# First mixer of a diffusion trunk: the scans' small PSUM tiles alternate between two banks, one of them the bank of the finishing transposes

## The chip, the cores and the metric

The kernel is one program on one core of a Trainium2 chip. The metric is the device time of one execution in microseconds (us). Before the change it is 3440.08 us, the median of three runs (3439.80 to 3440.29). The core's engines are PE (TensorE: matmuls and transposes), DVE (VectorE), ACT (ScalarE), POOL (GpSimd) and SP (SyncE, which here only issues DMAs). Each runs its own queue of instructions strictly in order and waits for the others on semaphores.

## The reference, cut to what matters

The trunk has two layers over 1280 tokens (256 of a prompt and 1024 latents). The change lies in the mixer of the first one, which runs two scans beside each other, each forwards and backwards, on one input projection:

```python
def mlstm_scan(q, k, v, log_i, log_f, C0, n0, m0):
...
        s = jnp.einsum('bthd,bshd->btsh', qc, kc) * jnp.exp(dmat - m_t[:, :, None, :])
        w_inter = jnp.exp(inter - m_t)
        num = jnp.einsum('btsh,bshv->bthv', s, vc) + w_inter[..., None] * jnp.einsum('bthd,bhdv->bthv', qc, C)
...
        C = keep[..., None, None] * C + jnp.einsum('bsh,bshd,bshv->bhdv', wg, kc, vc)
...
def ssd_scan(x, dt, A, Bm, Cm, S0):
...
        w = jnp.einsum('btgn,bsgn->btsg', Cc, Bc)[..., None] * decay * dtc[:, None]
        y = (jnp.einsum('btsgr,bsgrp->btgrp', w, xc)
             + jnp.einsum('btgn,bgrpn->btgrp', Cc, S) * jnp.exp(acum)[..., None])
...
        S = jnp.exp(a_last)[..., None, None] * S + jnp.einsum('bsgr,bsgrp,bsgn->bgrpn', wS, xc, Bc)
...
def even_mixer(h, w_in, ...):
...
    qk, v, o, ig, fg, z, xbc, dt = _split(h @ w_in, EVEN_SIZES)
    qk = jax.nn.silu(dwconv(qk, conv_a_w, conv_a_b)).astype(F32)
...
    ha = group_rms(ha, NH_A, a_norm_w).astype(h.dtype)
...
    yb = group_rms(y, NG_B, b_norm_w).astype(h.dtype)
    out = jnp.concatenate([ha, yb], axis=-1) @ w_out
```

Behind it stand an MLP, the second layer's attention mixer and another MLP, which the change does not touch.

## The kernel before

`Even.run` computes the first mixer. It walks through four pairs of scans: `ssd(0)`, `mlstm(0)`, `ssd(1)`, `mlstm(1)` and so on; an `ssd(i)` is two heads of the state-space scan, an `mlstm(h)` one head of the other. Each scan takes the 1280 tokens in ten chunks of 128 and both directions at once. In a first pass over the chunks, `key(c)` transposes the keys of a chunk on PE (tile `pk` or `pb`), ACT scales them out of PSUM, and `state(c)` multiplies them into the chunk's contribution to the state. In a second pass, `weights(c)` computes the 128x128 product of queries and keys (`pS` or `pG`), DVE multiplies it into the decay matrix of that chunk (`bcm` or `bcs`: sent by DMA, masked by DVE, exponentiated by ACT), and one step later `rows(c-1)` multiplies the matrix of the chunk before with the values (`pn` or `pny`). `ssd` also transposes the start states (`s0p`) and, when the second pass has reached the end of a direction, the final state (`sfp`, `final`), which ACT copies out (`so`).

When a group of four chunks (or the last two) has all its rows, it is normalised and `finish` transposes it (`fps`, up to four transposes into one bank), and ACT scales it out (`ob`); the last mLSTM head and the last SSD pair instead split it into two parts for the next matmul (ACT `hh`, then DVE `hl`).

Between all these small steps PE runs the input projection of what comes next: `self.gap()` pulls a few matmuls (`mmf`, `mmt`) out of `self.stream` after each step. PE's order there is written out by hand, since the scheduler is told to leave PE alone:

```python
            with net.pool("eu2") as self.u2, net.pool("es") as self.sp:
                with self.tc.manual_schedule(engines=PE_ONLY):
                    for i in range(4):
                        j = i // 2
```

The orders of ACT, DVE, POOL and SP are the scheduler's. After the block, the second pass of the last head, `mlstm(3, X)`, runs as `for _ in self.last: self.gap()`, and there the scheduler orders PE too. That stretch, about 725 to 794 us of the trace, is called the tail here; it ends where the output projection's matmuls (`o`) begin.

PSUM has eight banks of 512 fp32 columns. The pool of this mixer, opened as `net.pool("eps", 1, psum=True)`, gives three to the projection (tag `mm`), two to the rows (`n`), one to the states (`c`), one to the finishing transposes (`tp`: `fps`, `sfp`), and one to the small tiles (`s`: `pk`, `pS`, `s0p`, `pb`, `pG`). A tag with one buffer means that the next tile of the tag may be written only when the last reader of the one before has finished. Line numbers are those of the kernel before; from L1475 on, the changed kernel's are 4 higher.

Of the kernel before, what the change touches and what calls it, by code (L numbers as in the profile page):

```python
# [9 lines left out]
F32 = mybir.dt.float32  # L10
# [6 lines left out]
P = 128  # L17
# [978 lines left out]
class Even:  # L996
# [18 lines left out]
    def proj_feat(self, hi, lo, m, sink):  # L1015
        for g, (o, n, s) in enumerate(GROUPS):
            ps = self.pp.tile([P, 512], F32, tag="mm", name="mmf", bufs=3)
            self.net.gemm(ps[:m, :n], lambda k: (hi[:, k, :m], lo[:, k, :m]), lambda k: self.h[g][k], range(KD))
            sink(g, ps[:m, :n])

    def w_feat(self, col):
        hi = self.wp.tile([P, KD, P], F32R, tag="wh", name="wf_hi")
        lo = self.wp.tile([P, KD, P], F32R, tag="wl", name="wf_lo")
        raw = self.raw([P, KD, P])
        self.nc.sync.dma_start(raw, self.a["w_in_even"][0, :, col:col + P].rearrange("(k p) f -> p k f", p=P))
        self.split_w(raw, hi, lo)
        return hi, lo
# [431 lines left out]
    def mlstm(self, h, X=None):  # L1459
        nc, V, sp, pp = self.nc, self.nc.vector, self.sp, self.pp  # L1460
# [14 lines left out]
        kw = {}  # L1475

        def key(c):
            pk = pp.tile([P, 512], F32, tag="mm", name="pk", bufs=3) if X else pp.tile([P, P], F32, tag="s", name="pk", bufs=1)
            nc.tensor.transpose(pk[:, :P], kT[:, c * P:(c + 1) * P], self.net.ident)
            kw[c] = sp.tile([P, 2, P], F32, tag="kw", name="kw", bufs=2)  # L1480
            for d in range(2):
                nc.scalar.activation(kw[c][:, d, :], pk[:, :P], AF.Copy, scale=col(1, d, c))
# [22 lines left out]

        def weights(c):
            p0 = c * P
            pS = pp.tile([P, P], F32, tag="s", name="pS", bufs=1)
            nc.tensor.matmul(pS, kT[:, p0:p0 + P], qT[:, p0:p0 + P], start=True, stop=True)
            b = bc[c]  # L1510
            V.tensor_tensor(b[:, 0], pS.unsqueeze(1).to_broadcast([P, 2, P]), b[:, 0], ALU.mult)
            (nc.gpsimd if BQ else V).tensor_tensor(b[:, 1], qT[:, p0:p0 + P].unsqueeze(1).to_broadcast([P, 2, P]), b[:, 1], ALU.mult)
# [23 lines left out]
        for c in range(NT + 1):  # L1536
            if c < NT:
                key(c)
                yield 1
            if c > 0:  # L1540
                state(c - 1)
                yield 1
# [29 lines left out]
    def ssd(self, i):  # L1572
        net = self.net
        nc, V, sp, pp = self.nc, self.nc.vector, self.sp, self.pp
# [11 lines left out]
        for q in range(0, NT, 3):  # L1586
            ps = pp.tile([P, 3, P], F32, tag="n", name="xps", bufs=2)
# [6 lines left out]
            self.gap(XG)  # L1594
        for d in range(2):
            c0, c1 = ORDERS[d][0][0], ORDERS[d][1][0]
            ps = pp.tile([P, P], F32, tag="s", name="s0p", bufs=1)
            nc.tensor.transpose(ps, s0[:, d], self.net.ident)
            nc.scalar.copy(S[d][:, c0, :], ps)
            nc.gpsimd.memset(S[d][:, c1, :], 0.0)  # L1600
            self.gap(XG)
# [2 lines left out]
        bt, xw = {}, {}  # L1604

        def key(c):
            pb = pp.tile([P, P], F32, tag="s", name="pb", bufs=1)
            nc.tensor.transpose(pb, BT[:, c * P:(c + 1) * P], self.net.ident)
            bt[c] = sp.tile([P, P], F32, tag="bt", name="bt", bufs=2)
            nc.scalar.copy(bt[c], pb)  # L1610
            xw[c] = sp.tile([P, 2, 2, 64], F32, tag="kw", name="xw", bufs=2)
            (nc.gpsimd if XW else V).tensor_tensor(xw[c], x4(c), cb(c, 2), ALU.mult)
# [12 lines left out]
        for c in range(NT + 1):  # L1625
            if c < NT:
                key(c)
                self.gap()
            if c > 0:
                state(c - 1)  # L1630
                self.gap()
# [25 lines left out]

        def weights(c):
            p0 = c * P
            pG = pp.tile([P, P], F32, tag="s", name="pG", bufs=1)  # L1660
            nc.tensor.matmul(pG, BT[:, p0:p0 + P], CT[:, p0:p0 + P], start=True, stop=True)
            b4 = bc[c].rearrange("p d h t -> p (d h) t")
            V.tensor_tensor(b4, b4, pG.unsqueeze(1).to_broadcast([P, 4, P]), ALU.mult)
            xd[c] = sp.tile([P, 2, 2, 64], F32, tag="xd", name="xd", bufs=2)
            (nc.gpsimd if XD else V).tensor_tensor(xd[c], x4(c), cb(c, 1), ALU.mult)
# [62 lines left out]
    def run(self, fills=((), (), (), ())):  # L1728
        nc, net = self.nc, self.net
        self.wp = net.enter(net.pool("ew", EW, side="right"))  # L1730
        with net.pool("eu") as self.up, net.pool("ec") as cp, net.pool("eps", 1, psum=True) as self.pp:
            slots = cycle(range(4))
            u = lambda: self.up.tile([P, T], F32, tag=f"u{next(slots)}", name="raw_u", bufs=1)
            rings = cycle((lambda: self.raw([P, D]), lambda: u()[:, :D]))
            self.h = net.first(lambda: next(rings)(), self.pp)
            self.free, self.U, self.where, self.held, self.todo = list(range(4)), {}, {}, [], []
            self.pulled = self.done = 0
            self.credit = self.ratio = 0.0
            B = lambda j: self.channel("B", 2576 + 512 + j * P, 12 + j, self.bcs[j, 0])
            C = lambda j: self.channel("C", 2576 + 768 + j * P, 14 + j, self.bcs[j, 1])  # L1740
            x = lambda i: self.channel("x", 2576 + i * P, 8 + i)
            q = lambda i: self.channel("q", i * P, i)
            k = lambda i: self.channel("k", 512 + i * P, 4 + i)
            items = [B(0), x(0), C(0)]
            need, self.zdone = [], []
            for i in range(4):
                need.append(len(items) - (i % 2 == 0))
                items += [self.project_zv(i), q(i), k(i)]
                self.zdone.append(len(items) - 2)
                need.append(len(items))  # L1750
                if i % 2 == 0:
                    items += [self.project_o(i // 2), x(i + 1)]
                elif i == 1:
                    items += [B(1), x(2), C(1)]
            steps = self.adas(fills[2])
            items[MIX[0]:] = [self.mixed(t, steps, MIX[1]) for t in items[MIX[0]:]]
            items += [self.rest(steps), (lambda: None, self.early)]
            self.work = self.stream(items)
            with net.pool("er") as rp:
                self.setup(cp, self.pp, rp)  # L1760
                self.gates(rp)
                self.rows_ssd(rp)
                self.rows_mlstm(rp)
                nc.sync.dma_start(self.KS, self.keepd.partition_broadcast(P))
            self.pull(PULL)
# [4 lines that stand above are left out]
                        self.finish_items(need[2 * i])  # L1770
                        self.ratio = RATIO[2 * i]
                        if i % 2:
                            nc.sync.dma_start(self.take("C"), self.bcs[j, 1])
                        self.ssd(i)
                        self.finish_items(need[2 * i + 1])
                        self.ratio = RATIO[2 * i + 1]
                        if i % 2 == 0:
                            nc.sync.dma_start(self.take("B"), self.bcs[j, 0])
                        if i < 3:
                            for w in self.mlstm(i):  # L1780
                                self.gap(w)
                    while self.pull(1):
                        pass
                    while self.todo:
                        self.gap()
                for _ in self.last:
                    self.gap()
                while self.todo:
                    self.gap()
                us = iter(self.free[:NU])  # L1790
                u = lambda: next((self.up.tile([P, T], F32, tag=f"u{q}", name="ox_raw", bufs=1) for q in us), None) or self.u2.tile([P, NT, 130], F32, tag="C", name="ox_raw", bufs=CB).rearrange("p c f -> p (c f)")[:, :T]
                if OB == 1:
                    net.out_begin(self.a["w_out_even"][0], self.mixo, EVEN_K, 5, lambda: self.raw([P, D]), u)
                for _ in self.adas(FILLS[4], True):
                    pass
                if OB == 0:
                    net.out_begin(self.a["w_out_even"][0], self.mixo, EVEN_K, 5, lambda: self.raw([P, D]), u)
                net.leave(1)
# [818 lines left out]
```

## Time and profile before

| | |
|---|---|
| median of three runs | 3440.08 us (3439.80 to 3440.29) |
| the profiled execution | 3443.51 us, its span 3441.7 us |
| mean granted clock of PE in it | 0.975 |
| first mixer's scans, manual part | about 120 to 725 us of the span |
| its tail, to the output projection | about 725 to 794 us |
| the rest (output projection, MLP, second layer) | 794 to 3441.7 us |

The profiled execution is one single run and 3.4 us longer than the median. All durations below come from it. The trace's clock is a share of PE's full speed: 1.00 stands for 2.4 GHz and 0.50 for 1.2 GHz.

### The profile page before, as it was taken

How to read it: one execution, taken by the hardware profiler on the slowest of the kernel's cores; microseconds unless marked ns; L12 is line 12 of the kernel's file. 1: busy time of each engine (PE TensorE's matmuls, PEld its weight loads, DVE VectorE, ACT ScalarE, POOL GpSimd, SP SyncE). 2: the span in 40 equal slices, each digit the busy share in tenths (PEclk: the TensorE clock that was granted, in tenths of full speed). 3: DMA queues.
4: the chain of work that ended last, by engine and by line, in shares of the span. 5: the costliest groups of instructions: out<-in, count | busy, mean ns of one | idle time of the engine just before them, and what ended most of it. 6: DMA issues, size and time to landing. Idle time of an engine off the chain costs nothing. (4 is left out here: it accounts for less than half of the span.)

```text
span 3441.7 us, 50028 instructions
## 1 busy us (share of the span) xinstructions
PE 3250.1 (94%) x17997; PEld 2645.0 (77%) x17997; DVE 2236.0 (65%) x4130; ACT 1635.7 (48%) x3829; POOL 603.7 (18%) x977
## 2 busy tenths in 40 slices
PE   7898989979999999999969999999999999999998
PEld 4788778857888888888748776666678888888887
DVE  4665856664588877787635366666655866656666
ACT  4444544444544444434534466555555444444443
POOL 2323432321111110001211142000001111100112
PEclk8999999979999999999979999999999999999999
DMA  6334343265345546664432221000143443355544
GB/s 213 74 102 115 98 137 94 81 162 174 110 154 183 173 174 219 185 196 152 154 113 72 74 68 35 1 9 8 39 158 113 160 147 137 136 194 173 159 136 174
DMA packets 319460, 435.25 MB, mean 126 GB/s; under 512 B 29900, under 2 KB 210476, under 8 KB 319212
## 3 DMA queue, kind: packets, MB, share of 16 engines
q1 hardware_dynamic: 296620, 343.17, 32.5%
q0 software_dynamic: 22592, 88.89, 6.8%
q8 instruction: 141, 2.31, 0.3%
q14 instruction: 107, 0.88, 0.1%
HBM read 309.55 MB, written 122.43 MB: 126 GB/s over the span
## 5 line engine op out<-in xcount | busy, mean ns | idle before, releaser
L193 PE MATMUL y<-oph 128*128 128x512 f32 x896 | 348.7, 389 | 1.7 <-DVE y L724 1.7
L195 PE MATMUL y<-oph,opl 128*128 128x512 f32 x896 | 348.6, 389 | 0.0
L194 PE MATMUL y<-opl,oph 128*128 128x512 f32 x896 | 348.6, 389 | 0.0
L199 DVE TENSOR_TENSOR opl<-sa,oph 128x512 fp32r<-128x512 f32 x216 | 158.8, 735 | 167.2 <-ACT oph L198 166.9
L198 ACT CAST oph<-sa 128x512 fp32r<-128x512 f32 x216 | 133.9, 620 | 259.3 <-PE y L194 178.0
L193 PEld LDWEIGHTS y<-oph 128*128 128x128 f32 x896 | 168.2, 188 | 37.2 <-DVE y L724 2.1
L194 PEld LDWEIGHTS y<-opl,oph 128*128 128x128 f32 x896 | 168.2, 188 | 35.1
L195 PEld LDWEIGHTS y<-oph,opl 128*128 128x128 f32 x896 | 168.2, 188 | 34.8
L479 POOL DMA_DIRECT2D hd<-x x96 | 52.2, 544 | 645.5 <-ACT x L481 497.2
L193 PE MATMUL mmf<-hh,wf_hi 128*128 128x512 f32 (+1 forms) x384 | 152.5, 397 | 0.0
L1065 DVE SCALAR_TENSOR_TENSOR u<-pre,cw,u 128x510 f32<-128x510 f32 (+2 forms) x192 | 145.4, 766 | 9.7 <-ACT u L1063 8.5
L193 PE MATMUL mmt<-wt_hi,hh 128*128 128x256 f32 x480 | 149.7, 312 | 0.0
L194 PE MATMUL mmf<-hl,wf_hi 128*128 128x512 f32 (+1 forms) x384 | 139.3, 363 | 0.0
L195 PE MATMUL mmf<-hh,wf_lo 128*128 128x512 f32 (+1 forms) x384 | 139.3, 363 | 0.0
L194 PE MATMUL mmt<-wt_lo,hh 128*128 128x256 f32 x480 | 137.5, 286 | 0.0
L195 PE MATMUL mmt<-wt_hi,hl 128*128 128x256 f32 x480 | 137.3, 286 | 0.0
L204 POOL TENSOR_SCALAR rs_v<-ss 128x1 f32<-128x1 f32 x85 | 30.1, 354 | 496.6 <-ACT junk L956 347.6
L193 PE MATMUL o<-wh,hh 128*128 128x512 f32 x280 | 112.0, 400 | 0.0
L194 PE MATMUL o<-wl,hh 128*128 128x512 f32 x280 | 109.3, 390 | 0.7 <-DVE wl L199 0.7
L195 PE MATMUL o<-wh,hl 128*128 128x512 f32 x280 | 109.5, 391 | 0.0
L1993 PE MATMUL pom<-PTm,mla_h 128*64 128x256 f32 x336 | 106.5, 402 | 2.4 <-DVE ob L2005 2.0
L405 ACT ACTIVATE x<-x 128x512 f32<-128x512 f32 x112 | 70.3, 628 | 78.7 <-DVE x L638 60.5
(1081 smaller groups left out, 10240.3 us busy)
## 6 DMA issues: line engine op xcount, KB each, us to landing
sa<-hd SPq DMA_DIRECT2D x108, 512.0 KB
hd<-s POOLq DMA_DIRECT2D x128, 320.0 KB, 3.0
hd<-x POOLq DMA_DIRECT2D x96, 320.0 KB, 2.5
wh<-in_w_down SPq DMA_DIRECT2D x40, 512.0 KB
wl<-in_w_down SPq DMA_DIRECT2D x40, 512.0 KB
w_raw<-in_w_ada SPq DMA_DIRECT2D x32, 512.0 KB
wh<-in_w_up SPq DMA_DIRECT2D x30, 512.0 KB
wl<-in_w_up SPq DMA_DIRECT2D x30, 512.0 KB
```

What stands on the lines that cost most here:

```text
L193: mm(ps, lh, rh, start=first and j == 0, stop=False)
L194: mm(ps, lh, rl, start=False, stop=False)
L195: mm(ps, ll, rh, start=False, stop=last and j == n - 1)
L198: self.nc.scalar.copy(hi, raw)
L199: self.nc.vector.tensor_tensor(lo, raw, hi.bitcast(F32), ALU.subtract)
L204: nc.gpsimd.tensor_scalar(v, ss, scale, eps, ALU.mult, ALU.add)
L405: relu = lambda o, i: nc.scalar.activation(o, i, AF.Relu)
L479: store = lambda i, z: nc.gpsimd.dma_start(hd[p, i], z)
L1065: nc.vector.scalar_tensor_tensor(us, pre[:, i:i + e - a], cw[:, b, j + i:j + i + 1], us, ALU.mult, ALU.add)
L1993: self.nc.tensor.matmul(self.po[64 * b:64 * b + 64, 0], self.odd.Vm[(0 if self.big else 10) + 2 * i + b][:, 64 * self.h:64 * self.h + 64], ...
```

## The change

A new method hands out the small tiles. Each is a whole bank, of which the first 128 columns are used, and its tag alternates: the first tile goes to `s`, the second to `tp`, the third to `s`, whatever the tile is. `fps` and `sfp` stay on `tp` and are not counted in the turns.

```diff
@@ class Even
+    def small(self, name):
+
+        return self.pp.tile([P, 512], F32, tag=next(self.banks), name=name, bufs=1)[:, :P]
+
...
-            pk = pp.tile([P, 512], F32, tag="mm", name="pk", bufs=3) if X else pp.tile([P, P], F32, tag="s", name="pk", bufs=1)
+            pk = pp.tile([P, 512], F32, tag="mm", name="pk", bufs=3) if X else self.small("pk")
...
-            pS = pp.tile([P, P], F32, tag="s", name="pS", bufs=1)
+            pS = self.small("pS")
...
-            ps = pp.tile([P, P], F32, tag="s", name="s0p", bufs=1)
+            ps = self.small("s0p")
...
-            pb = pp.tile([P, P], F32, tag="s", name="pb", bufs=1)
+            pb = self.small("pb")
...
-            pG = pp.tile([P, P], F32, tag="s", name="pG", bufs=1)
+            pG = self.small("pG")
...
             self.pulled = self.done = 0
+            self.banks = cycle(("s", "tp"))
             self.credit = self.ratio = 0.0
```

PE's instructions and their order stay the same up to the tail; only what they wait for changes. On ACT, DVE, POOL and SP the scheduler moves some instructions by a few places throughout the mixer.

The first place is PE in the second pass of `mlstm(0)`: the small tile of one chunk, a step of projection, and the rows of the chunk before. Before:

```order
L195 MATMUL mmf_2717<-hh0_6_297,wf_lo_2241 128x512
L1509 MATMUL pS_2787<-u_1791,u_2096 128x128 [waits DVE_49]
L193 MATMUL mmf_2717<-hh0_7_299,wf_hi_2240 128x512
L194 MATMUL mmf_2717<-hl0_7_300,wf_hi_2240 128x512
L195 MATMUL mmf_2717<-hh0_7_299,wf_lo_2241 128x512
L1517 MATMUL pn_2806<-vx_2255,bcm_2673 128x129 [waits Activation_49]
```

And now:

```order
L195 MATMUL mmf_2717<-hh0_6_297,wf_lo_2241 128x512
L1513 MATMUL pS_2787<-u_1791,u_2096 128x128 [waits PE_49]
L193 MATMUL mmf_2717<-hh0_7_299,wf_hi_2240 128x512
L194 MATMUL mmf_2717<-hl0_7_300,wf_hi_2240 128x512
L195 MATMUL mmf_2717<-hh0_7_299,wf_lo_2241 128x512
L1521 MATMUL pn_2806<-vx_2255,bcm_2673 128x129 [waits DVE_49,Activation_49]
```

Nothing moved; the wait for DVE's multiplication went from the small tile to the rows behind it.

The second place is PE in the second pass of `ssd(0)`, where the final state's transpose `sfp` stands directly before a small tile `pG`, whose turn is `tp`. Before:

```order
L195 MATMUL mmf_1812<-hh1_4_421,wf_lo_1238 128x512
L1692 MATMUL sfp_1853<-ident_60,finS_1217 128x128 [waits Activation_49]
L1661 MATMUL pG_1866<-u_1138,u_895 128x128 [waits DVE_49]
L193 MATMUL mmf_1812<-hh1_5_423,wf_hi_1237 128x512
L194 MATMUL mmf_1812<-hl1_5_424,wf_hi_1237 128x512
```

And now:

```order
L195 MATMUL mmf_1812<-hh1_4_421,wf_lo_1238 128x512
L1696 MATMUL sfp_1853<-ident_60,finS_1217 128x128 [waits PE_49,Activation_49]
L1665 MATMUL pG_1866<-u_1138,u_895 128x128 [waits Activation_49]
L193 MATMUL mmf_1812<-hh1_5_423,wf_hi_1237 128x512
L194 MATMUL mmf_1812<-hl1_5_424,wf_hi_1237 128x512
```

Nothing moved; `pG` now waits for ACT, which is the copy of the `sfp` in front of it. The same stands at all eight `sfp` and, with `pS`, `pb` or `pk` behind `fps`, at most of the finishing transposes.

The third place is PE in the tail, at its first finishing transposes. Before:

```order
L1513 MATMUL pS_8022<-u_7228,u_7457 128x128 [waits DVE_49]
L1521 MATMUL pn_8026<-vx_7700,bcm_7994 128x129
L1522 MATMUL pn_8026<-C0_7703,bcm_7994 128x129 [waits DMAHW7_49,DMAHW6_49,Pool_49]
L1521 MATMUL pn_8026<-vx_7700,bcm_7994 128x129
...
L1448 MATMUL fps_7964<-ident_60,yS_7328 128x128 [waits DVE_49]
L1448 MATMUL fps_7964<-ident_60,yS_7328 128x128
L1513 MATMUL pS_8043<-u_7228,u_7457 128x128 [waits DVE_49]
```

And now (`pS_8022` is the second chunk's, `pS_8043` the third's):

```order
L1448 MATMUL fps_7964<-ident_60,yS_7328 128x128 [waits DVE_49]
L1448 MATMUL fps_7964<-ident_60,yS_7328 128x128
L1521 MATMUL pn_8026<-vx_7700,bcm_7994 128x129 [waits DVE_49]
...
L1513 MATMUL pS_8147<-u_7228,u_7457 128x128 [waits DVE_49]
L265 MATMUL ada031_8331<-w_raw_8332,cs_92 32x512 [waits DMAHW2_49]
L1513 MATMUL pS_8022<-u_7228,u_7457 128x128 [waits DVE_49]
```

The second chunk's `pS`, whose turn is `tp`, moved behind all six finishing transposes of the SSD pairs, and the third, fifth and seventh chunk's, on `s`, moved ahead of it.

## Rows read from the trace of the kernel before

**Rows 1.** The span in stretches (columns in the second line).
```profile
core 0: us, PE busy (x) PEld busy (x) DVE busy (x) ACT busy (x) POOL busy (x), PEclk, DMA share, GB/s
590.00:725.00 135.00, 117.01 (x786) 107.90 (x785) 86.22 (x213) 63.58 (x210) 39.73 (x61) 0.92 0.34 96
725.00:800.00 75.00, 52.22 (x282) 32.99 (x282) 44.02 (x124) 32.93 (x107) 16.27 (x23) 0.82 0.70 201
800.00:3441.70 2641.70, 2562.01 (x13500) 2055.42 (x13498) 1737.83 (x2963) 1257.38 (x2691) 362.42 (x616) 0.99 0.38 127
```

**Rows 2.** PE's waits, 120 to 725 us: releaser, total us, times, longest.
```profile
PE pS L1509 <- DVE bcm L1511: 21.5, 6, 6.3
PE pk L1479 <- ACT kw L1482: 7.4, 3, 3.6
...
PE pG L1661 <- DVE bcs__5462 L1663: 2.5, 1, 2.5
...
PE pn L1517 <- DVE bcm L1511: 1.8, 1, 1.8
...
PE fps L1444 <- ACT ob L1451: 1.2, 1, 1.2
...
PE pn L1517 <- DVE hA L1524: 0.7, 1, 0.7
...
PE pG L1661 <- DVE bcs__7332 L1663: 0.4, 1, 0.4
```

**Rows 3.** PE in order, second pass of `mlstm(0)`: start, us, instruction, wait before.
```profile
258.38 0.38 PE L1509 MATMUL pS<-u 128*128 128x128 f32 x2
...
259.29 0.38 PE L1517 MATMUL pn<-vx,bcm 128*128 128x129 f32 x2
...
266.21 0.79 PE L1509 MATMUL pS<-u 128*128 128x128 f32 x2 [4.48 <-DVE bcm L1511]
...
268.09 0.63 PE L1517 MATMUL pn<-vx,bcm 128*128 128x129 f32 x2
```

**Rows 4.** DVE in the same stretch.
```profile
264.95 0.61 DVE L1503 SCALAR_TENSOR_TENSOR bcm<-bcm,GM,maskadd 128x128 f32<-128x128 f32 x2 [6.51 <-DMA bcm<-mrows]
...
265.75 0.42 DVE L1511 TENSOR_TENSOR bcm<-pS,bcm 128x256 f32<-128x256 f32 x1
```

**Rows 5.** PE at the first and the last `sfp`.
```profile
179.62 0.27 PE L1692 MATMUL sfp<-ident,finS 128*128 128x128 f32 x1
179.73 0.39 PE L1661 MATMUL pG<-u 128*128 128x128 f32 x2
...
698.41 0.27 PE L1692 MATMUL sfp<-ident,finS 128*128 128x128 f32 x1
698.52 0.39 PE L1661 MATMUL pG<-u 128*128 128x128 f32 x2
```

**Rows 6.** ACT at the same two places.
```profile
180.68 0.24 ACT L1694 COPY so<-sfp 128x128 f32<-128x128 f32 x1
...
700.44 0.25 ACT L1694 COPY so<-sfp 128x128 f32<-128x128 f32 x1
```

**Rows 7.** The finishing transposes of 622.8 us: PE, DVE and ACT.
```profile
622.82 0.60 PE L1444 MATMUL fps<-ident,hA 128*128 128x128 f32 x4
623.32 0.49 PE L1509 MATMUL pS<-u 128*128 128x128 f32 x2
...
623.18 3.53 DVE L1065 SCALAR_TENSOR_TENSOR u<-pre,cw,u 128x514 f32<-128x514 f32 x2
...
627.53 0.68 ACT L1451 ACTIVATE ob<-fps,nw 128x512 f32<-128x512 f32 x1
```

**Rows 8.** PE's waits in the tail, 725 to 800 us.
```profile
PE ada L265 <- DMA w_raw<-in_w_ada: 10.8, 4, 8.1
PE fps L1444 <- DVE hl L1448: 4.3, 3, 1.6
PE pS L1509 <- DVE bcm L1511: 2.7, 1, 2.7
```

## The prediction

> **What bounds the kernel now.** I read the span in stretches first, then PE's waits, then the orders of PE, DVE and ACT at the places those waits name. From 800 us to the end PE is busy 2562.0 of 2641.7 us [rows 1], and the change reorders nothing there, so what the mixer gains or loses reaches the end of the kernel undiminished. From 590 to 725 us PE is busy 117.0 of 135 us, and in the tail 52.2 of 75 [rows 1]: PE carries the scans too, but there it waits. The change can act on PE's waits of 120 to 725 us [rows 2] and on the tail.
>
> The waits that belong to the one small bank are those of `pS` on DVE's multiplication (21.5 us in 6), of `pk` on ACT's `kw` (7.4 in 3) and of `pG` on DVE (five, from 2.5 down to 0.4, together 5.9) [rows 2]. That is 34.8 us in 14 waits, about 1% of the kernel. A second bank takes away the cause that the trace names for all of them. The question is what is late next, and what the second bank's other user costs.
>
> **What the removed waits are worth.** Take the wait of 4.48 us before `pS` at 266.21 [rows 3]. It ends when DVE has multiplied the `pS` before it, 265.75 + 0.42. But DVE was late itself: its mask-add had sat 6.51 us for the DMA of `bcm` [rows 4]. The rows of that same chunk read the same product, and they follow one projection step later, at 268.09 [rows 3]. With a second bank, `pS` and the step run ahead of the wait, and the rows wait instead. What is gained is the work that moves ahead: at full clock `pS` and a step took 259.29 - 258.38 = 0.91 us [rows 3]. After the wait they took 1.88, since the granted clock had dropped; but the clock would be low after the wait at the rows as well, for the work that then comes, so I count 0.91 and keep 1.88 as the upper end. By the same reading of the six `pS` waits: two at 0.9, two short ones whole (1.0 each, since a step lies between), and two with about two steps in between at 1.6 and 1.9. Together 7.3 of 21.5. The two long `pk` waits are followed by `state`, which needs the `kw` that ended the wait; two half steps move ahead, 0.85 each, and the short third is counted whole: 2.0 of 7.4. The `pG` waits are shorter than the way to the rows that need the product, and I count them whole: 5.9. Sum of the gains: 15 us. Ends: 10 (if the `pG` waits too move on by half) and 21 (if the moved work counts with its elapsed time at the low clock).
>
> **What the second bank's other user costs.** PE's order stays as it is written, and in it a finishing transpose is often followed at once by a small tile whose turn is `tp`. That tile must wait until ACT has emptied the transposes just written. Nobody waited for those copies before, so ACT came to them when its queue allowed. At the first `sfp`, `pG` ran at 179.73 and the copy `so` only ended at 180.68 + 0.24 = 180.92: 1.19 us. At the last, 698.52 against 700.69: 2.17 us [rows 5, 6]. There are eight such places, all with `pG`, and they run from 0.73 to 3.27 us, 15.6 together. They come in pairs, one per direction; the second `sfp` of a pair is itself moved back by the wait at the first, while the exponentials ahead of `so` on ACT hang on DMAs and DVE, so of the second ones (8.2 together) I count 4.5, and of the first 7.3 all: 11.8.
>
> `fps` is worse, since its copy stands behind `hA` and the convolution's work. At 622.82 four transposes are written and `pS` follows at 623.32, but `ob` ends at 628.21, because ACT stood behind a `den` that DVE computed only after two convolution steps of 3.53 us: 4.89 us [rows 7]. Three such places (`pS` behind `fps` at the last chunk of heads 0 to 2) cost 9.0 us; a wait that PE had anyway right behind goes off (1.8 of `pn` on `bcm`, 0.7 of `pn` on `hA` [rows 2]), and some of the waits at the next SSD's start, so I count 6.0. Three places with `pb` behind the last, two-transpose `fps` cost 0.68 each: 2.0. In head 1, where six `fps` and the `pk` of the first pass interleave, four waits of 0.5 to 2.1 us make 3.9; 1.2 of `fps` on `ob` was there before [rows 2], so 2.5. Sum of the new waits: 22 us of 30.5 raw. The low end is a bank emptied as soon as written: about 0.25 us of copy and a start for each `sfp` (0.43 with the overlap), 0.7 to 0.9 for `ob`, in all 11.
>
> Behind each of these waits stands everything PE has queued, the projection above all, and behind that ACT's `pre` and DVE's convolutions of the next head, so a microsecond lost on PE comes back only where PE later waits for something that does not hang on it. The only such waits of size are those for DMAs, and I have counted no relief there.
>
> **The tail.** Here the scheduler orders PE too. Odd chunks' `pS` take their turn in the bank through which nine finishing transposes go, each followed by `hh` and `hl` on ACT and DVE (PE waits 4.3 us for `hl` in three cases [rows 8]); so the second chunk's `pS` now stands behind six of them, and the rows of chunks 1 to 4 come in a clump. Against that, even chunks run ahead, and the tail's longest wait, 8.1 of the 10.8 us for `w_raw` [rows 8], is for a DMA that covers a good part of it. Going through the new order with the durations of before, the output projection's first matmul comes 3 us earlier to 3 us later than now, up to 5 if the clump meets that DMA. I take +1.
>
> **The sum.** -15 + 22 + 1 = +8 us on the profiled execution of 3443.5, that is 3451.5. That execution is 3.4 us above the median of the runs, so 3448 us for the median.
>
> **A rule against this reading.** In the trace the wait at `pS` goes back to a late DMA [rows 4], not to the bank. The Trainium skill, Perfetto Trace Analysis, section Matmuls, says that independent matmul groups should rotate through different PSUM banks so that the emptying of one overlaps the next group's matmuls, which is what this change does. By that rule all 14 waits would go. And PSUM — Partial Sum Buffer, section Summary: rules for kernel authors, says "Evacuate promptly"; the eight copies `so` that nobody had to hurry are where this kernel does not, and this second rule speaks for the cost.
>
> **The rivals.** (a) *Faster: ACT empties the shared bank at once.* ACT is far from full, and if its order lets `so` and `ob` run as soon as the transposes are done, the new waits fall to their low end of 11. With gains of 21 and a tail at 0 that is -10, 3430 us. It decides when the new waits stay under about 13. Against it: ACT's order keeps the exponentials ahead of `so` at nearly all places, and `ob` behind `hA`. (b) *All removed waits go for good*, 34.8 us with new waits at 22: -13, 3427 us; with rows that wait for the same product I give it 0.03. It is the time that the rule of the section Matmuls would lead to. (c) *No change:* the new waits are partly taken out of the waits that the removed ones turn into, since both end with DVE: 15 against 15, 3440 us. (d) *Slower by more:* the raw 30.5 us stand, the gains are 12, and the tail pays 3: +21, 3461 us. It decides if each PE delay makes the next copy late as well.
>
> **How the numbers follow.** My forecast, the new waits outweighing the old by 4 to 14 us (3444 to 3454), gets 0.46; (c) 0.20, (a) 0.17, (b) 0.03, (d) 0.14. A measurement of this kernel can tell about 0.2% from no change, 6.9 us: from 3433.2 to 3447.0. A third of the forecast's chance lies below 3447, so: slower 0.30 + 0.14 = 0.44, same 0.16 + 0.20 = 0.36, faster 0.20. For the range I leave out (b), the outer half of (a) and what of (d) lies above 3461: 3432 to 3461.
>
> **What would show it.** Right: `pG` waiting for ACT's `so` at all eight `sfp`, 0.5 to 3 us each; `pS` behind `fps` waiting for `ob`; no `pS` or `pk` waiting for its own kind any more, but `pn` waiting for DVE's `bcm` and `pc` for ACT's `kw`, with 10 to 20 us between them; the output projection starting some 8 us later. Wrong: the waits on `so` and `ob` together under 13 us, or `pn` waiting far less than `pS` did, or a tail whose length changes by more than 5 us.

## The result, and the profile after

The changed kernel takes 3478.34 us in the median of four runs (3474.69 to 3480.65), beside 3440.18 us before on the same chip: a ratio of 1.0110 with a 95% interval of 1.0095 to 1.0125. A second group of runs of it gave 1.0115 (1.0098 to 1.0132). So it is about 38 us slower, where 8 us were forecast and 3461 us was the upper end of the range: the sign was right, the size was not.

Where the time went is read by marks that every trace has: the first `s0p` (start of the manual part), the last `sfp`, and the twenty-first matmul of the output projection, by which its late start is over. All times are from PE's rows in order, in us. The tail so marked begins some 27 us before the one of the front part, which starts at 725 us.

| stretch | before | after | after, second profile |
|---|---|---|---|
| start to the first `s0p` | 137.9 | 142.8 | 135.6 |
| first `s0p` to last `sfp` (manual part) | 560.5 | 571.4 | 566.8 |
| last `sfp` to 21st output matmul (tail) | 101.6 | 119.0 | 121.5 |
| the rest, difference to before | 0 | +3.9 | -2.5 |

The first and the last line differ in sign between the two profiles and hold the same instructions in the same order: they are scatter. The manual part is 6 to 11 us longer, the tail 17 to 20 us.

PE's waits in the manual part of the changed kernel (releaser; us in total, times, longest), which answer to [rows 2]:

```profile
PE pG L1665 <- ACT so L1698: 11.5, 7, 2.2
PE pn L1521 <- DVE bcm L1515: 9.0, 3, 4.1
PE pS L1513 <- ACT ob L1455: 8.4, 3, 5.3
PE pc L1493 <- issue: 7.9, 2, 4.0
PE pn L1521 <- DVE hA L1528: 5.3, 4, 2.5
...
PE pn L1521 <- DVE den L1525: 3.1, 1, 3.1
PE pk L1483 <- ACT ob L1455: 2.4, 2, 1.2
PE pb L1612 <- ACT ob L1455: 1.7, 3, 0.6
```

No `pS`, `pk` or `pG` waits for its own kind any more. In their place the rows wait for DVE (`pn` on `bcm`, `hA`, `den`: 17.4 us, where before it was 2.5), the state product waits at the two places where `pk` had waited for `kw` (`pc`, 7.9 us, by the profile without a releaser), and the small tiles wait for ACT: `so` at seven of the eight final states within this stretch, 11.5 us, the eighth right behind it with 2.2, and `ob` 8.4 + 2.4 + 1.7.

The three kinds of place in order. First the `pS` of [rows 3], PE's rows:

```profile
266.08 0.38 PE L1513 MATMUL pS<-u 128*128 128x128 f32 x2
...
270.23 0.46 PE L1521 MATMUL pn<-vx,bcm 128*128 128x129 f32 x2 [3.08 <-DVE den L1525]
```

`pS` now runs at once, the projection step behind it too, and then the rows wait 3.08 us: DVE still sits for the DMA of `bcm`. Of 4.48 us, 1.40 were gained, between the 0.91 and the 1.88 us of `pS` and a step in [rows 3]. Second the final state of [rows 5], third the finishing transposes of [rows 7], PE's rows:

```profile
185.09 0.49 PE L1665 MATMUL pG<-u 128*128 128x128 f32 x2 [2.03 <-ACT so L1698]
...
638.82 0.79 PE L1513 MATMUL pS<-u 128*128 128x128 f32 x2 [5.29 <-ACT ob L1455]
```

and ACT's at the same two places, answering to [rows 6, 7]:

```profile
184.79 0.24 ACT L1698 COPY so<-sfp 128x128 f32<-128x128 f32 x1
...
638.09 0.68 ACT L1455 ACTIVATE ob<-fps,nw 128x512 f32<-128x512 f32 x1
```

`pG` starts as soon as the copy `so` has ended, `pS` as soon as `ob` has; the longest wait was read as 4.89 us and is 5.29.

In the tail PE's waits from the last `sfp` to the 21st output matmul read, before (two lines that [rows 8] leaves out) and after:

```profile
PE fps L1444 <- DVE hA L1440: 2.5, 2, 1.5
...
PE fps L1444 <- DVE yS L1440: 0.6, 1, 0.6
```

```profile
PE fps L1448 <- DVE hA L1444: 12.7, 3, 5.5
...
PE fps L1448 <- DVE yS L1444: 5.1, 1, 5.1
PE fps L1448 <- DVE hl L1452: 4.7, 3, 1.6
PE o L193 <- ACT wh L198: 3.8, 1, 3.8
```

The wait of 8.1 us for `w_raw` is gone, but the finishing transposes of the last head wait 12.7 us for their normalised rows (2.5 before), the first ones 5.1 us (0.6), and the output projection runs out of weights six matmuls after its start:

```profile
820.48 0.77 PE L193 MATMUL o<-wh,hh 128*128 128x512 f32 x1
...
827.17 0.79 PE L193 MATMUL o<-wh,hh 128*128 128x512 f32 x1 [3.79 <-ACT wh L198]
```

The last chunk's `pS` shows what the new order of PE does. Its turn is `tp`. Before, it ran ahead of the second group of the last head's finishing transposes, and now it stands right behind them. Before:

```profile
775.12 0.39 PE L1509 MATMUL pS<-u 128*128 128x128 f32 x2
...
784.93 0.66 PE L1444 MATMUL fps<-ident,hA 128*128 128x128 f32 x4 [1.51 <-DVE hA L1440]
```

and after:

```profile
807.27 1.11 PE L1448 MATMUL fps<-ident,hA 128*128 128x128 f32 x4 [3.09 <-DVE hA L1444]
...
810.17 0.80 PE L1513 MATMUL pS<-u 128*128 128x128 f32 x2
```

Counted from the last `sfp` (698.4 and 714.1 us), that `pS` comes at 96 us instead of 77, DVE's normalisation of the last group of rows at 105 instead of 88, and the first load of the output weights at 108 instead of 91.

### The profile page after: what moved, and what is told of

It reads as the page before. It is cut to its first block, busy times and chain, and to the rows that moved or that the text cites. A ratio compares the mean times of both kernels' runs of the same rounds, so it can differ in the third digit from the quotient of the medians.

```text
span 3478.8 us, 50126 instructions
## 1 busy us (share of the span) xinstructions
PE 3269.0 (94%) x17997; PEld 2656.3 (76%) x17997; DVE 2239.5 (64%) x4130; ACT 1638.5 (47%) x3829; POOL 604.4 (17%) x977
## 5 line engine op out<-in xcount | busy, mean ns | idle before, releaser
L195 PEld LDWEIGHTS y<-oph,opl 128*128 128x128 f32 x896 | 168.2, 188 | 35.1
L194 PE MATMUL o<-wl,hh 128*128 128x512 f32 x280 | 110.5, 395 | 0.5 <-DVE wl L199 0.5
L1998 PE MATMUL pom<-PTm,mla_l 128*64 128x256 f32 x336 | 107.0, 403 | 0.0
## 6 DMA issues: line engine op xcount, KB each, us to landing
sa<-hd SPq DMA_DIRECT2D x108, 512.0 KB
wh<-in_w_down SPq DMA_DIRECT2D x40, 512.0 KB
wl<-in_w_down SPq DMA_DIRECT2D x40, 512.0 KB
w_raw<-in_w_ada SPq DMA_DIRECT2D x32, 512.0 KB
wh<-in_w_up SPq DMA_DIRECT2D x30, 512.0 KB
wl<-in_w_up SPq DMA_DIRECT2D x30, 512.0 KB
```

The costliest lines, as they stand in the source:

```text
L194: mm(ps, lh, rl, start=False, stop=False)
L195: mm(ps, ll, rh, start=False, stop=last and j == n - 1)
L1998: self.nc.tensor.matmul(self.po[64 * b:64 * b + 64, 0], self.odd.Vm[(0 if self.big else 10) + 2 * i + b][:, 64 * self.h:64 * self.h + 64], ...
```

## The experiments

Theory A: the loss is PE waiting, in its written order, for the copies out of the shared bank, plus the tail. Theory B: it comes from the other order that the scheduler gives to DVE, ACT, POOL and SP as soon as tiles alternate. The kernels of one group were run beside the same runs of the kernel before, so only ratios are compared (0.1% is 3.4 us). A difference between two ratios is good to some 5 to 7 us by the intervals. Each profiled execution gives the two stretches of the table above:

| kernel | ratio (95%) | manual part | tail |
|---|---|---|---|
| before | 1 | 560.5 | 101.6 |
| changed | 1.0110 (1.0095 to 1.0125) | 571.4 | 119.0 |
| changed, again | 1.0115 (1.0098 to 1.0132) | 566.8 | 121.5 |
| e1_flip | 1.0021 (1.0011 to 1.0031) | 548.4 | 110.5 |
| e2_tail_s | 1.0047 (1.0032 to 1.0061) | 569.9 | 100.1 |
| e3_tail_only | 1.0044 (1.0029 to 1.0058) | 559.5 | 113.5 |
| e4_sfp_c | 1.0037 (1.0024 to 1.0050) | 552.2 | 113.5 |
| e5_sc | 0.9955 (0.9942 to 0.9967) | 544.3 | 93.2 |
| e6_flip_tail_s | 0.9982 (0.9971 to 0.9992) | 549.4 | 98.8 |
| e7_last_s | 1.0053 (1.0039 to 1.0066) | 554.9 | 113.2 |
| e8_sfp_c_tail_s | 0.9990 (0.9980 to 0.9999) | 552.5 | 92.3 |
| e9_sc_tail | 0.9986 (0.9973 to 0.9998) | 545.4 | 105.6 |
| e10_sc_sn | 0.9952 (0.9936 to 0.9968) | 541.2 | 96.2 |
| e11_pS_only | 0.9974 (0.9963 to 0.9985) | 551.7 | 96.6 |

One profile's stretch is good to some microseconds only: the manual part of the kernel before is held unchanged by two others (559.5 and 554.9 beside its 560.5), and the tail's pS stand on one bank in seven (92.3 to 101.6). Prices are therefore taken from the ratios where a pair of kernels gives them.

**The turns the other way round.**

```diff
-            self.banks = cycle(("s", "tp"))
+            self.banks = cycle(("tp", "s"))
```

> The turns start with the other bank, so that at the finishing transposes and the final states of the manual part the small tile that follows stands on the bank of its own. Theory A (the cost is PE waiting in its written order for the copies out of the shared bank, plus the tail): the 26 us of waits of pG, pS, pk and pb on so and ob fall to under 6 us, the rest of the manual part keeps the gain of about 11 us, the tail and the output projection's start stay late by 10 to 15 us; 3440 to 3450 us. Theory B (the cost is the scheduler's other order on DVE, ACT, POOL and SP, whatever bank a tile stands on): 3465 to 3480 us.

Measured: 3440.64 us, ratio 1.0021, 31 us better than the changed kernel by moving every tile to the other of the same two banks. Here the tile behind each `sfp` stands on its own bank, and `sfp` itself waits for DVE instead (1.1 and 0.9 us at two places); in the manual part

```profile
PE pn L1521 <- DVE bcm L1515: 7.9, 3, 4.0
...
PE s0p L1602 <- ACT ob L1455: 4.8, 3, 3.2
...
PE sfp L1696 <- DVE bcs__5553 L1667: 1.1, 1, 1.1
...
PE pk L1483 <- ACT ob L1455: 0.6, 1, 0.6
```

all that is left of waiting for `ob` is 4.8 us of `s0p`, 0.6 of `pk`, and 1.9 of `fps` itself. The manual part is 12 us shorter than before instead of 11 longer, as A had it. But the scheduler's order came back too. Matched by name, in order of time, at least 97 of DVE's 841 instructions in the manual part and 62 of ACT's stand out of the order of before in the changed kernel, and 6 and 6 in this one. So this run takes away the waits and most of the other order together, and does not part A from B there. What speaks for A is that PE's waits in the manual part for anything but `so` and `ob` are 30.6 us in the changed kernel, 35.1 in this one and 48.4 before: the other order made those no longer. Nor are the waits for `so` in the changed kernel, 13.7 us at all eight places, longer than the lateness of 15.6 us that the prediction read from the kernel before.

**The tail's `pS` back on one bank, and only the tail's `pS` alternating.**

```diff
-            pS = self.small("pS")
+            pS = pp.tile([P, 512], F32, tag="s", name="pS", bufs=1)[:, :P] if X else self.small("pS")
```

> As changed, but the weights tiles of the last mLSTM head stay on their own bank, as before the change; the manual part is that of the change. Theory A: the tail and the start of the output projection come back to what they were, the manual part keeps its +14 us; 3452 to 3460 us. Theory B (orders, not the tail's bank): less than 5 us off the changed kernel, 3470 us or more.

The reverse keeps `pk`, `s0p`, `pb`, `pG` and the other heads' `pS` on the tag `s`:

```diff
-            pS = self.small("pS")
+            pS = self.small("pS") if X else pp.tile([P, 512], F32, tag="s", name="pS", bufs=1)[:, :P]
```

> The reverse: only the last mLSTM head's weights tiles alternate, all others stay on their own bank. Theory A: the manual part is that of before, tail and output projection cost about 14 us; 3450 to 3458 us. Theory B: within 5 us of the kernel before.

Measured: 1.0047 and 1.0044, that is 16 us for the manual part alone and 15 us for the tail alone, as A had them. Together they are 31 of the 38 us; the tail costs 22 when the manual part has the change too (1.0110 less 1.0047), which is not clear of the 15 by the intervals.

**The final states' transposes on a bank that is idle in that pass.**

```diff
-            ps = pp.tile([P, 512], F32, tag="tp", name="sfp")
+            ps = pp.tile([P, 512], F32, tag="c", name="sfp", bufs=1)
```

> As changed, but the final states' transposes go to the bank of the state products, which nothing uses in that pass. Theory A: the eight waits of pG on so (13.7 us) go, all else stays; 10 to 14 us under the changed kernel, 3462 to 3468 us. Theory B: under 4 us off the changed kernel.

Measured: 1.0037, 25 us off the changed kernel: A by sign, but nearly twice its size. The eight waits of `pG` for `so` are gone; of the others some shrink and some grow (the wait of `pc` was 7.9, those of `pn` on `bcm` 9.0, of `pS` and `pk` on `ob` 8.4 and 2.4). In the manual part:

```profile
PE pS L1513 <- ACT ob L1455: 9.5, 3, 5.6
PE pn L1521 <- DVE bcm L1515: 6.5, 3, 3.4
PE pk L1483 <- ACT ob L1455: 5.3, 2, 4.1
...
PE pc L1493 <- issue: 4.4, 2, 3.0
```

All of PE's waits there fall from 54.8 to 42.7 us, and the time in which PE is busy with the same matmuls from 516.4 to 509.3, at a mean granted clock of 0.97 instead of 0.96; the tail is 5.5 us shorter.

The same edit with the tail kept on one bank separates the two:

```diff
-            ps = pp.tile([P, 512], F32, tag="tp", name="sfp")
+            ps = pp.tile([P, 512], F32, tag="c", name="sfp", bufs=1)
...
-            pS = self.small("pS")
+            pS = pp.tile([P, 512], F32, tag="s", name="pS", bufs=1)[:, :P] if X else self.small("pS")
```

> As changed, with the final states' transposes on the bank of the state products and the tail's weights tiles on their own. Theory A: the manual part 8 us shorter than before, tail as before; 6 to 10 us under the kernel before. Theory B (they trade): 0 to 8 us over it.

Measured: 0.9990, 3 us under before, and so 20 us under the kernel whose code differs from it only in the bank of `sfp` (1.0047). Less than the 6 to 10 us that A expected, on its side of zero by little. The bank of eight copies of 0.24 us is worth 20 to 25 us by these two pairs, where the waits in the trace add up to 13.7 (14.6 in the second profile). The two profiles of the second pair show where the rest is. The manual part is 17.4 us shorter, of which 10.4 are waits for `so`, 3.8 other waits of PE, and 3.2 its busy time with the same matmuls (515.2 to 512.0). The tail is 7.8 us shorter; there the last wait for `so`, 2.2 us, and a wait of 5.9 us of the first finishing transposes for `yS` are gone. But the scheduler's order differs too between the two (at least 70 of DVE's 841 instructions in the manual part), so how much of what goes beyond the waits for `so` belongs to the bank is not shown.

**The turns the other way round, and the tail on one bank.**

```diff
-            self.banks = cycle(("s", "tp"))
+            self.banks = cycle(("tp", "s"))
...
-            pS = self.small("pS")
+            pS = pp.tile([P, 512], F32, tag="s", name="pS", bufs=1)[:, :P] if X else self.small("pS")
```

> The turns start with the other bank, and the tail's weights tiles stay on their own. Theory A: the manual part 12 us shorter, as in the run with the turns the other way round, tail and output projection as before; 10 to 14 us under the kernel before. Theory B (tail and manual part trade with each other): within 4 us of the kernel before.

Measured: 0.9982, 6 us under before; neither A's 10 to 14 nor B's 4. The interval (0.9971 to 0.9992) leaves room for both. The profile shows 11 us in the manual part, of which the ratio confirms about half.

**Two banks without sharing.**

```diff
-            self.banks = cycle(("s", "tp"))
+            self.banks = cycle(("s", "c"))
...
-            pG = self.small("pG")
+            pG = self.small("pG") if i < 3 else pp.tile([P, 512], F32, tag="s", name="pG", bufs=1)[:, :P]
...
-            pS = self.small("pS")
+            pS = pp.tile([P, 512], F32, tag="s", name="pS", bufs=1)[:, :P] if X else self.small("pS")
```

and `pk`, `s0p`, `pb` on the tag `s`.

> No tile shares the bank of the finishing transposes: the weights tiles pS and pG of the manual part alternate between their own bank and that of the state products, which is idle in that pass; all other small tiles, the last SSD pair's pG and the tail's pS stay on their own bank. Theory A (two banks are worth 12 to 13 us in the manual part, and the rest was the shared bank): no wait on so or ob but the one that was there before, the manual part 8 to 12 us shorter, tail as before; 8 to 12 us under the kernel before. Theory B (the gains move on to the rows entirely): within 4 us of the kernel before.

Measured: 0.9955, 3419.11 beside 3435.25 us, 15 us better than before and more than A expected. No small tile waits for `ob` or `so`; the rows wait 17.4 us for DVE, as in the changed kernel, and `pS` waits for nothing:

```profile
PE pn L1521 <- DVE bcm L1515: 8.2, 4, 2.6
PE pk L1483 <- ACT kw L1486: 7.5, 3, 3.8
PE pn L1521 <- DVE hA L1528: 6.8, 5, 3.0
...
PE pn L1521 <- DVE den L1525: 2.4, 1, 2.4
```

ACT and DVE keep the order of before here (at most 3 of 841 instructions elsewhere), as they nearly do in e6_flip_tail_s. Of the two e6_flip_tail_s is 9 us slower, and in its manual part the waits for `ob` and of `sfp` for DVE are 8.3 us longer: with the order held, sharing the finishing bank costs about the length of the waits.

Two variants divide that gain by kinds. With `pG` on one bank:

```diff
-            pG = self.small("pG") if i < 3 else pp.tile([P, 512], F32, tag="s", name="pG", bufs=1)[:, :P]
+            pG = pp.tile([P, 512], F32, tag="s", name="pG", bufs=1)[:, :P]
```

> Only pS of the manual part alternates (own bank and that of the state products); pG stays on one. Theory A (the pS waits move on to the rows but for 7 to 9 of 21.5 us): the manual part 7 to 10 us shorter than before. Theory B (they go entirely): 14 us or more. Theory C (they move on entirely): under 3 us.

and with the key transposes alternating as well, over the rows' banks, which the first pass leaves idle:

```diff
+    def early_small(self, name):
+        t = next(self.banks2)
+        return self.pp.tile([P, 512], F32, tag=t, name=name, bufs=2 if t == "n" else 1)[:, :P]
...
-            pk = pp.tile([P, 512], F32, tag="mm", name="pk", bufs=3) if X else pp.tile([P, 512], F32, tag="s", name="pk", bufs=1)[:, :P]
+            pk = pp.tile([P, 512], F32, tag="mm", name="pk", bufs=3) if X else self.early_small("pk")
...
-            pb = pp.tile([P, 512], F32, tag="s", name="pb", bufs=1)[:, :P]
+            pb = self.early_small("pb")
...
-            self.banks = cycle(("s", "c"))
+            self.banks, self.banks2 = cycle(("s", "c")), cycle(("s", "n"))
```

> As the kernel in which pS and pG alternate between their own bank and that of the state products, and the first pass's key transposes pk and pb alternate between their own bank and the rows' two banks, which are idle in that pass. Theory A (the pk waits of 7.4 us are worth about 2, since the state product needs the same kw): 0 to 3 us under that kernel. Theory B (worth most of their length): 5 to 7 us under it.

Measured: 0.9974 for `pS` alone, 9 us for waits of 21.5, A's amount; so `pG` is worth 6 to 7 more (1.0 and the like for waits of 5.9), and `pk` with `pb` 1 us on top (0.9952; the profile's manual part is 3 us shorter), with the intervals overlapping in both steps. `pS` and `pk` are as A had them. At 3420.78 beside 3434.80 us this last kernel and e5_sc beat both the kernel before and the changed one, and can't be told apart.

**What in the tail costs it.** Two runs. In the first the last chunk's `pS` is taken out of the turns:

```diff
-            pS = self.small("pS") if X else pp.tile([P, 512], F32, tag="s", name="pS", bufs=1)[:, :P]
+            pS = self.small("pS") if X and c < NT - 1 else pp.tile([P, 512], F32, tag="s", name="pS", bufs=1)[:, :P]
```

> Only the last head's weights tiles alternate, and of these the last chunk's stays on its own bank. Theory A (the output projection starts badly because the last chunk's pS, the last reader of the q and k buffers, is late, and the load of the mixed rows into one of these buffers stands ahead of the output weights on SP): the 7 us between the output projection's first and twentieth matmul fall to under 1.5, the tail keeps up to 5; 2 to 7 us over the kernel before. Theory B (the late weights come from the tail's length, whichever pS is late): the 7 us stay; 10 to 15 us over the kernel before.

Measured: 1.0053, no better than with the last chunk in turn, and the output projection still runs dry. The theory that the last `pS` holds the buffer into which the mixed rows are loaded is not borne out: the load no longer waits for `pS` (9.8 us in e3_tail_only), though 5.3 us for POOL's multiplication of the same chunk, and leaves 89 us after the last `sfp` instead of 93; but the weights' load leaves at 102 instead of 103. SP's rows of this run, in its tail:

```profile
780.67 0.34 SPq L831 DMA_DIRECT2D ox_raw<-mixo  x1
793.82 1.29 SPq L824 DMA_DIRECT2D ow_raw<-in_w_out_even  x3
```

and PE's, at the output projection:

```profile
798.48 0.80 PE L193 MATMUL o<-wh,hh 128*128 128x512 f32 x1 [3.86 <-ACT wh L198]
```

The weights' load waited 13.1 us for DVE's split of the mixed rows (`hl`), most of which stands in DVE's queue behind the last head's normalisation; and that came 99 us after the last `sfp` instead of 88. Before, the weights' load waited 3.1 us for it. SP's waits, before and in this run:

```profile
SPq L824 <- DVE hl L199: 3.1, 1, 3.1
```

```profile
SPq L824 <- DVE hl L199: 13.4, 2, 13.1
...
SPq L831 <- POOL bcm L1516: 5.3, 1, 5.3
```

In the second run the tail's `pS` alternate too, but over the bank of the state products. These end some 33 us after the last `sfp`, ahead of the second chunk's `pS`, and nothing else uses the bank behind them:

```diff
-            pS = pp.tile([P, 512], F32, tag="s", name="pS", bufs=1)[:, :P] if X else self.small("pS")
+            pS = self.small("pS")
```

> The kernel in which pS and pG alternate between their own bank and that of the state products, with the tail's pS alternating between these two as well. Theory A (the tail's loss comes from the odd chunks standing in the bank of the finishing transposes): last final state to twentieth output matmul as in the kernel where the tail keeps one bank, within 4 us; 3415 to 3425 us beside a kernel before of 3435. Theory B (any alternation lets the scheduler reorder the tail to its loss): 10 us or more longer from there, 3427 us or more.

Measured: 0.9986, 11 us worse than with one bank (0.9955). B's side of the expectation, though the tail's stretch, 105.6 us, is nearer to the 92 to 102 of the tails on one bank than to the 113 to 122 of those that alternate over the finishing bank from the second chunk on. In its tail there is no wait for `wh`, and the finishing transposes wait 1.9 us for their rows, where with the shared bank alone (e3_tail_only) it is

```profile
PE fps L1448 <- DVE hA L1444: 7.2, 2, 5.0
...
PE o L193 <- ACT wh L198: 3.8, 1, 3.8
```

So some 11 us (5 to 17 by the intervals) of the tail's 15 to 22 go with the order that the scheduler gives it as soon as `pS` has two banks. The rest, 4 to 11 us, would be the finishing bank's, and is not clear of the noise. Which instruction's move makes the first part wasn't found.

**A second look at the changed kernel**, the same code once more:

> The changed kernel a second time, to part what belongs to the change from the scatter of the first 70 us, where both kernels issue the same instructions. Theory A (the change costs in the manual part and from there to the twentieth output matmul): these two stretches again 9 to 12 and 14 to 19 us longer than before, the first stretch within 5 us either way and the rest within 4; ratio 1.006 to 1.010. Theory B (the whole 37 us of the first profile belong to it): 5 us again at the start and 4 at the end; ratio 1.011.

Measured: 1.0115, so the ratio stands as B had it, and the stretches speak for A: -2.3 at the start, +6.3 in the manual part (less than the 9 to 12 expected), +19.9 in the tail, -2.5 in the rest. The two profiles of the changed kernel differ by 5 us in a manual part of the same order, so one profile beside another is a poor measure of 10 us; the profile of before, at 3443.5 us, was itself above most of the times of that kernel (medians of 3433 to 3435 us in the later groups of runs), by some in the tail.

## Why the prediction was wrong

- **What is gained.** Right. The sum said 15 us, between 10 and 21; the kernels that alternate over unshared banks gain 15 to 16. `pS` was sized at 7.3 and is worth 9, `pG` at 5.9 and 6 to 7, `pk` at 2.0 and about 1. The reason was right too: the wait moves on to the rows, which need the same product of the same late DMA. Rival (b), by which all 14 waits go, is wrong by a factor of two. By that the Trainium skill's rule to rotate matmul groups through banks (Perfetto Trace Analysis, section Matmuls) holds in sign with e5_sc (0.9955), and buys about 45% of the waits that carry the bank's name.
- **What the shared bank costs.** The places and their releasers were right, one by one. The size was not: 22 us counted, of 30.5 raw. The kernel with the change in the manual part alone is at +16 us and the unshared one at -16, so the price is about 32 us. In length the waits came out at 26.2 us: 13.7 for `so` (11.8 counted; the second of a pair is shorter in only two of the four pairs, 5.3 us in all where 4.5 were counted), 8.4 for `pS` on `ob` (6.0 counted, since waits that PE "had anyway" right behind were taken off), 4.1 for `pk` and `pb` (4.5). So the step that failed here is the size of this term: 4 us too short in the waits' length, and a price of some 6 us beyond that, about what a difference of two ratios is good to.

  Waits for `ob` cost their length: 9 us for 8.3 in e6_flip_tail_s beside e5_sc, 13 for 13.0 in e8_sfp_c_tail_s beside e10_sc_sn, with little or some of the scheduler's order changed (6 and 27 of DVE's 841 instructions against before). The waits for `so` cost 20 to 25 us for 13.7, in kernels whose order on DVE differs more, so that excess stays open. What the sum of the collisions put at nothing is PE's busy time: the same matmuls of the manual part take 515.2 us with the shared bank (e2_tail_s) and 507.5 without (e5_sc), at granted clocks of 0.96 and 0.97. The prediction allowed a higher price only as rival (d). The Trainium skill says "Evacuate promptly" (PSUM — Partial Sum Buffer, section Summary: rules for kernel authors) and gives PSUM's small size as the reason. In this trace the price of a late copy is a held bank: six of the eight copies of 0.24 us start about 2 us after their transposes.
- **The tail.** This is the step that failed most: +1 us, with +5 as its end, where the change costs 15 us there alone and 22 together with the rest. The new order was read with the durations of before for PE, and the clump of rows and the queue of finishing transposes were seen; but ACT's and DVE's queues behind them were not followed. The normalisation of the last head, which the finishing transposes wait for, and the split of the mixed rows, which the output weights wait for, both stand in DVE's order, and both came 17 to 18 us later. The last chunk's `pS`, 19 us later, is not the whole cause: with that tile on its own bank (e7_last_s) the loss stays. Some 11 us come with two banks of any kind (e9_sc_tail), and which move makes them stays open.
- **The sum.** -16, +32 and +22 make +38, the measured difference, as they must, being differences of the same ratios. With the raw value for the collisions and the tail at its upper end the same reading would have given about +20.
- **The rivals.** (d), raw waits and a tail that pays, was the nearest, with 21 us and a chance of 0.14; (a) and (c) needed the collisions under 15 us.
- **The signs in the profile** named ahead were right, but for the tail: `pG` on `so` at all eight places between 0.35 and 2.2 us, `pS` on `ob`, `pn` on `bcm` and `pc` waiting 16.9 us between them (10 to 20 were named). The tail's 17 us more is the sign of being wrong that came true.

## What to carry to other kernels

A buffer that alternates is worth the work that can run before the next consumer of the same late product, not the wait that carries the buffer's name: go on to the next instruction that needs the same product before counting a gain. Look at the second bank's other tenant in the in-order engine's written order: a tile directly behind it waits for a copy that nobody hurried until then. Here, with the tail on one bank, the choice of banks made the difference between 16 us lost, 6 us gained by the other parity, and 15 us gained with an idle bank. Count, too, how far the scheduler's order on the other engines moves from one variant to the next, before a difference is put down to the bank alone. Where a scheduler orders a stretch, follow the queues of all engines to the load that the next stage needs, and take the longer end.

## What the runs showed that was not expected

In the first 35 us both kernels have the same order of instructions on every engine, and yet the two profiles differ by 4 to 5 us there. PE's rows before:

```profile
17.42 0.60 PE L265 MATMUL ada<-raw_u,cs 128*32 128x512 f32 x2
17.62 0.60 PE L265 MATMUL ada<-w_raw,cs 128*32 128x512 f32 x2
```

and after:

```profile
18.54 1.06 PE L265 MATMUL ada<-raw_u,cs 128*32 128x512 f32 x2
18.55 1.06 PE L265 MATMUL ada<-w_raw,cs 128*32 128x512 f32 x2
```

A pair of the same matmuls takes 0.60 us in one execution and 1.06 in the other, until about 33 us. The trace's entries of the granted clock fit that: the first one starts at 14.7 us in the profile of before and at 33.3 us in that of the changed kernel (14.1 in its second profile). Until then the pairs take 1.06 to 1.07 us in all three, as they do under the entry of 0.50 from 21.5 to 24.9 us of the first, and under the entries of 1.00 they take 0.60 to 0.62. So PE ran at the lower level, 1.2 GHz, 19 us longer in that execution, though it was at the same matmuls in the same order. Why isn't known. A mean clock over a stretch without entries reads 1.00 all the same, as it does here from 16 to 32 us. The executions of the kernel before range from 3424 to 3445 us over all groups, so a change of 0.2% needs runs side by side, many of them.
